# Strassen's seven products in the gate and up stages of a two-layer trunk

## The chip, the cores and the metric

The kernel runs on one core of a Trainium2 chip. A core has TensorE (PE; its weight loads, PEld, are listed apart), VectorE (DVE), ScalarE (ACT), GpSimd (POOL) and SyncE (SP, which issues most transfers here). Each engine takes its own instructions in a fixed order; semaphores hold an instruction back until its operands are there. SBUF is the working memory, PSUM the eight banks into which TensorE accumulates. The metric is the time of one execution on the device, in microseconds.

## The reference

512 tokens of 1024 features go through two layers. In each a mixer (an SSD scan in layer 0, a gated MLP over chunks of 128 tokens in layer 1) adds to the residual h, then a feed-forward stage, then a gated embedding of a second input:

```python
h = h + mix
h = h + swiglu(rmsnorm(h, norm_ffn[i]), ffn_w_gate[i], ffn_w_up[i], ffn_w_down[i])
e = rmsnorm(p[i] @ ple_w_proj[i], ple_norm[i])
gate = jax.nn.sigmoid(rmsnorm(h, ple_gate_norm[i]) @ ple_w_gate[i])
h = h + gate * e
...
def swiglu(u, w_gate, w_up, w_down):
    return (jax.nn.silu(u @ w_gate) * (u @ w_up)) @ w_down
```

All is float32. The feed-forward width is 2816, that is 22 blocks of 128 features.

## The kernel before

The residual lives feature-major in SBUF: eight tiles `H[k]` of 128 features by 512 tokens. Every large product is done as three products of a narrower float32 form: each operand is split in hi + lo, and `mm3` (lines 264 to 267) adds hi*hi, hi*lo and lo*hi in PSUM.

**Weights.** `Weights` holds all weights in the order of their use. A raw tile `wraw` (1 MB, two buffers) is loaded on SP's queue; each of its units is split by ScalarE (`whi`, line 68) and VectorE (`wlo`, line 70) into one of three hi/lo buffers, two units ahead of TensorE (`get`, with raised priority for the planner that writes out each engine's order from priorities and from the program's order). For gate and up a unit is one block: 1024 contraction rows by 128 features.

**Norm.** `Norm.block(k)` scales `H[k]` by the norm's weight, splits it into `Xh[k]`, `Xl[k]` (lines 416, 417) and adds its square to a running sum (ScalarE, then GpSimd at line 350). 1/rms of the tokens, `rs`, is multiplied into what the products give; `stat` makes it at its first use (a product with ones, a root, a reciprocal at line 283).

**Feed-forward.** `ffn` walks over the 22 blocks in parts of 8, 8 and 6, two blocks of gate and then the same two of up at a time: a round. `gemm` takes a block's 8 contraction steps, 24 matmuls of 512 columns. `on_gate` (lines 749 to 752): times rs on VectorE, silu on ScalarE, times rs on GpSimd. `on_up` (line 758): times the gate, then `split`. After each part the down product adds to h (line 606). The norm that follows takes each block of h after the last part. Between rounds, a generator (`early`) takes one step of other work: in layer 0 the norm of the embedding E and the preparation of layer 1's spatial weights, in layer 1 the second embedding.

## Time and profile before

| | |
|---|---|
| time, median of 3 runs | 1579.58 us (1577.21 to 1579.68) |
| span of the profiled execution | 1576.3 us |
| TensorE / its weight loads | 1550.5 / 1281.1 us busy |
| VectorE | 902.4 us |
| ScalarE | 644.2 us |
| GpSimd | 294.6 us |
| granted TensorE clock, mean | 0.995 of 2.4 GHz |

The span runs from the first to the last instruction of one profiled execution, for which no time beyond the span is recorded; the median of the runs lies 3.3 us above it. A busy time is the union of an engine's instructions. Matmuls overlap in the record, so the distance between two starts tells more than the duration of one.

### The profile page before, as it was taken

Reading aid. Unit: us, or ns where it says so; the run is one execution under the profiler, and the core shown is the slowest. Engines: PE = TensorE matmul, PEld = TensorE weight load, DVE = VectorE, ACT = ScalarE, POOL = GpSimd, SP = SyncE. Lnnn points to the kernel's source line nnn. Section 1 sums busy time; section 2 is a strip of 40 time slices with the busy share of each in tenths; the row PEclk is TensorE's granted clock in tenths of the full one; section 3 lists DMA queues with packets and bytes.
Section 4 is the critical chain, followed back from the end, with each engine's and each line's share of the span. In section 5 each row is a group of like instructions: output and inputs, shape, how many; then the busy total and the mean of one; then the engine's idle time right before and its main releaser. Section 6 shows DMA issues by size and latency. Waiting matters only on the chain.

```text
span 1576.3 us, 18219 instructions
## 1 busy us (share of the span) xinstructions
PE 1550.5 (98%) x7348; PEld 1281.1 (81%) x7348; DVE 902.4 (57%) x1226; ACT 644.2 (41%) x843; POOL 294.6 (19%) x226
## 2 busy tenths in 40 slices
PE   7999999999999999999999999999999999999996
PEld 5878888888878788888888888888888888888885
DVE  5679895589886433433356657535544364433445
ACT  5556663466454212222245534323343242222335
POOL 3032220123155101100124200202221001101122
PEclk9999999999999999999999999999999999999999
DMA  6463443544433323323232332332223232332231
GB/s 181 116 142 101 128 127 107 127 127 107 133 97 113 106 80 107 99 89 107 75 112 81 107 113 81 100 107 94 92 95 106 82 107 89 98 107 81 80 107 54
DMA packets 151364, 164.15 MB, mean 104 GB/s; under 512 B 5320, under 2 KB 133872, under 8 KB 151280
## 3 DMA queue, kind: packets, MB, share of 16 engines
q1 hardware_dynamic: 149648, 157.74, 33.3%
q0 software_dynamic: 1600, 5.24, 1.2%
q8 instruction: 57, 0.93, 0.2%
q14 instruction: 27, 0.22, 0.0%
q10 hardware_dynamic: 32, 0.01, 0.0%
HBM read 160.75 MB, written 2.23 MB: 103 GB/s over the span
## 4 chain that ended last, share of the span: by engine, by line
PE 88%; DVE 6%; ACT 2%; DMA 2%; SPq 1%; POOL 1%; issue 1%; ACTq 0%; DVEq 0%; POOLq 0%
PE ps L265 28%; PE ps L266 28%; PE ps L267 28%; DVE wlo L70 1%; DMA csb<-cs_dram 1%; PE ps L872 1%; PE ps L527 1%; DVE csb L576 1%; PE ps L529 1%; PE ps L260 1%; DVE acc L451 1%; PE ps L583 1%; DVE csb L511 1%; POOL sq L350 0%; DVE xsT L957 0%
## 5 line engine op out<-in xcount | busy, mean ns | idle before, releaser
L68 ACT ACTIVATE whi<-wraw 128x1024 fp32r<-128x1024 f32 (+1 forms) x270 | 279.0, 1038 | 697.6 <-PE ps L266 616.8
L265 PE MATMUL ps<-xh,whi 128*128 128x512 f32 x1120 | 441.4, 394 | 2.0 <-ACT h L400 2.0
L266 PE MATMUL ps<-xl,whi 128*128 128x512 f32 x1120 | 437.0, 390 | 2.9 <-DVE xl L398 2.0
L267 PE MATMUL ps<-xh,wlo 128*128 128x512 f32 x1120 | 436.9, 390 | 0.0
L70 DVE TENSOR_TENSOR wlo<-wraw,whi 128x1024 fp32r<-128x1024 f32 (+1 forms) x268 | 328.4, 1230 | 99.4 <-ACT whi L68 98.2
L265 PE MATMUL ps<-gh,whi 128*128 128x512 f32 x784 | 306.3, 391 | 0.0
L266 PE MATMUL ps<-gl,whi 128*128 128x512 f32 x784 | 305.0, 389 | 0.0
L267 PE MATMUL ps<-gh,wlo 128*128 128x512 f32 x784 | 304.9, 389 | 0.0
L265 PEld LDWEIGHTS ps<-xh,whi 128*128 128x128 f32 x1120 | 210.8, 188 | 48.6 <-issue 3.0
L266 PEld LDWEIGHTS ps<-xl,whi 128*128 128x128 f32 x1120 | 210.8, 188 | 47.0 <-DVE xl L398 2.5
L267 PEld LDWEIGHTS ps<-xh,wlo 128*128 128x128 f32 x1120 | 210.7, 188 | 44.5
L752 POOL TENSOR_TENSOR zs<-zs,rs 128x512 f32<-128x512 f32 x44 | 74.1, 1687 | 545.3 <-ACT zs L751 545.3
L267 PEld LDWEIGHTS ps<-gh,wlo 128*128 128x128 f32 x784 | 147.2, 188 | 30.8
L606 DVE TENSOR_TENSOR h<-h,ps 128x512 f32<-128x512 f32 x88 | 60.1, 686 | 195.7 <-PE ps L267 195.6
L265 PEld LDWEIGHTS ps<-gh,whi 128*128 128x128 f32 x784 | 147.2, 188 | 30.4 <-issue 0.3
L266 PEld LDWEIGHTS ps<-gl,whi 128*128 128x128 f32 x784 | 147.3, 188 | 30.0
L758 DVE TENSOR_TENSOR xsT<-ps,zs 128x512 f32<-128x512 f32 x44 | 30.4, 691 | 126.6 <-PE ps L267 117.8
L749 DVE TENSOR_TENSOR acc<-ps,rs 128x512 f32<-128x512 f32 x44 | 30.4, 690 | 108.2 <-PE ps L267 108.2
L350 POOL TENSOR_TENSOR sq<-sq,sq 128x512 f32<-128x512 f32 x43 | 67.7, 1574 | 128.8 <-ACT sq L347 126.8
L266 PE MATMUL ps<-wlo,gh 128*128 128x512 f32 (+1 forms) x200 | 76.3, 381 | 1.7 <-DVE wlo L70 1.7
L265 PE MATMUL ps<-whi,gh 128*128 128x512 f32 (+1 forms) x200 | 76.4, 382 | 0.0
L267 PE MATMUL ps<-whi,gl 128*128 128x512 f32 (+1 forms) x200 | 76.1, 381 | 0.0
(293 smaller groups left out, 1425.0 us busy)
## 6 DMA issues: line engine op xcount, KB each, us to landing
wraw<-in_ffn_w_gate_dram SPq DMA_DIRECT2D x22, 1024.0 KB, 5.4
wraw<-in_ffn_w_up_dram SPq DMA_DIRECT2D x22, 1024.0 KB, 5.3
wraw<-in_ssd_w_in_dram SPq DMA_DIRECT2D x16, 1024.0 KB, 5.5
wraw<-in_ffn_w_down_dram SPq DMA_DIRECT2D x16, 1024.0 KB, 5.3
wraw<-in_gmlp_w_in_dram SPq DMA_DIRECT2D x16, 1024.0 KB, 5.8
wraw<-in_ssd_w_in_dram SPq DMA_DIRECT2D x16, 512.0 KB, 4.3
csb<-cs_dram SPq DMA_DIRECT2D x32, 256.0 KB, 4.2
wraw<-in_ple_w_gate_dram SPq DMA_DIRECT2D x8, 1024.0 KB, 5.2
```

Of the source, the lines that this page charges most:

```text
L68: nc.scalar.activation(hi, src, AF.Copy)
L70: (nc.vector if n > 1 else nc.gpsimd).tensor_tensor(lo, src, f32(hi), op=ALU.subtract)
L260: nc.tensor.transpose(ps, src, ident)
L265: mm(ps, wh, xh, start=start, stop=False)
L266: mm(ps, wh, xl, start=False, stop=False)
L267: mm(ps, wl, xh, start=False, stop=stop)
L350: nc.gpsimd.tensor_tensor(sq, sq, accum, op=ALU.add)
L451: stt(a[:, d:], ps[:, : S - d], pcols[:, 0, j * 32 + b : j * 32 + b + 1], a[:, d:], op0=ALU.mult, op1=ALU.add)
L606: tt(H[m], H[m], ps, op=ALU.add)
L749: tt(a, ps, rs, op=ALU.mult)
L752: nc.gpsimd.tensor_tensor(s, s, rs, op=ALU.mult)
L758: tt(t, ps, gate[m], op=ALU.mult)
```

## The change

The gate and up products of a pair of blocks (256 features, 1024 contraction rows, 512 tokens) are taken as a 2 by 2 product of quarters in Winograd's form of Strassen's algorithm: seven products of 128 features by 512 contraction rows by 256 tokens, each of 4 steps of three matmuls of 256 columns, instead of eight. The left sides are four quarters of the raw weights (A11 to A22) and four sums S1 to S4 that GpSimd makes, one pair ahead, in tiles that before held E. The right sides are quarters of x (B11 and so on) and sums T1 to T4 that `QuarterNorm.block` makes, once a layer. The hi/lo buffers are cut in halves, one for each of the seven left sides. The results are put together from PSUM by VectorE, with one copy on ScalarE, in `after`. E is stored in DRAM and read back; its norm, the preparation of layer 1's spatial weights and layer 1's embedding move from between the rounds to behind the blocks of the last down product. In each layer's first pair, five products go side by side, three contraction steps first. The diff, cut to its core:

```diff
+PRODUCTS = (("P1", "A11", "B11"), ("P6", "S2", "T2"), ("P7", "S3", "T3"), ("P5", "S1", "T1"),
+            ("P4", "A22", "T4"), ("P2", "A12", "B21"), ("P3", "S4", "B22"))
...
+    def add_pair(self, src, col):
+        r = len(self.raws)
+        v = src.rearrange("(k p) n -> p k n", p=P)
+        self.raws.append([[(lambda t: t.rearrange("p (k n) -> p k n", n=256), v[:, :, col : col + 256])], None])
+        for _, name, _ in PRODUCTS:
+            if self.units and isinstance(self.units[-1][1], str):
+                self.at.append(self.at[-1] + 1)
+            else:
+                self.at.append(self.at[-1] // 2 * 2 + 2)
+            self.units.append((r, name))
+        self.pairs.append(r)
+    def quarters(self, r):
+        v = self.raws[r][1].rearrange("p (k t n) -> p k t n", t=2, n=256)
+        return {f"A{i + 1}{t + 1}": v[:, :, t, i * P : (i + 1) * P] for i in range(2) for t in range(2)}
+    def add_sums(self, n):
+        if n in self.sums:
+            return
+        r = self.pairs[n]
+        self._load(r)
+        a = self.quarters(r)
+        s = {}
+        for j in range(4):
+            s[f"S{j + 1}"] = self.sum_tile(4 * (n % 2) + j).rearrange("p (k n) -> p k n", n=P)
+        add = self.nc.gpsimd.tensor_tensor
+        add(s["S1"], a["A21"], a["A22"], op=ALU.add)
+        add(s["S2"], s["S1"], a["A11"], op=ALU.subtract)
+        add(s["S3"], a["A11"], a["A21"], op=ALU.subtract)
+        add(s["S4"], a["A12"], s["S2"], op=ALU.subtract)
+        self.sums[n] = s
...
+            if isinstance(view, str):
+                i = self.pairs.index(r)
+                self.add_sums(i)
+                src = (self.quarters(r) | self.sums[i])[view]
+                if self.at[n] % 2 == 0:
+                    self.half = [self.hl_pool.tile([P, 1024], F32R, tag=t, name=f"{t}{n}") for t in ("whi", "wlo")]
+                o = self.at[n] % 2 * 512
+                hi, lo = (t[:, o : o + 512].rearrange("p (k n) -> p k n", n=P) for t in self.half)
+                nc.scalar.activation(hi, src, AF.Copy)
+                nc.vector.tensor_tensor(lo, src, f32(hi), op=ALU.subtract)
+                self.tiles[n] = (hi, lo)
+                self.split += 1
+                continue
...
+        if isinstance(self.units[i][1], str):
+            r = self.units[i][0]
+            if self.units[i][1] == "A11":
+                n = self.pairs.index(r) + 1
+                if n < len(self.pairs) and self.pairs[n] == r + 1:
+                    self.add_sums(n)
+            j = i
+            while j + 1 < len(self.units) and self.at[j + 1] // 2 < self.at[i] // 2 + self.bufs:
+                j += 1
+            self._split(j)
+            self.taken += 1
+            return self.tiles.pop(i)
...
-                if i and j == 8:
-                    add_proj(1)
-                add_cols(ffn_w_gate[i], j * P, KD, 256)
-                add_cols(ffn_w_up[i], j * P, KD, 256)
+                W.add_pair(ffn_w_gate[i], j * P)
+                W.add_pair(ffn_w_up[i], j * P)
             kb = part[1] - part[0]
             for m in range(4):
+                if i and part[1] == 22 and m == 2:
+                    add_proj(1)
...
+                nc.sync.dma_start(out=e_dram[m], in_=e)
...
+                E.append(slot(f"e{m}"))
+                nc.sync.dma_start(out=E[m], in_=e_dram[m])
...
+    class QuarterNorm(Norm):
+        def __init__(self, col):
+            super().__init__(col)
+            self.extra = iter(("CT", "CT", "xdt", "xdt", "xdd", "prev", "x3", "csb", "csb", "csb", "csb", "Btok"))
+            self.right = {name: [] for _, _, name in PRODUCTS}
+            self.x = None
+        def pieces(self, k, q):
+            if q < 2:
+                return xslot(2 * k + q)
+            return [work(next(self.extra), F32R) for _ in range(2)]
+        def add(self, src, hl, names):
+            split(src, *hl)
+            for j, name in enumerate(names):
+                self.right[name].append([t[:, j * HS : (j + 1) * HS] for t in hl])
+        def block(self, k):
+            self.accum = sq_accum(H[k], self.accum, k)
+            x = work("xsT" if k % 2 else "zs")
+            act(x, H[k], AF.Identity, scale=self.col(k))
+            if k % 2 == 0:
+                self.x = x
+                return
+            xa, xb, k2 = self.x, x, k // 2
+            a1, a2, b1, b2 = xa[:, :HS], xa[:, HS:], xb[:, :HS], xb[:, HS:]
+            t23 = work("zs")
+            if k2 % 2 == 0:
+                self.t4 = work("xsT")
+            self.add(xb, self.pieces(k2, 0), ("B21", "B22"))
+            tt(t23[:, HS:], b2, a2, op=ALU.subtract)
+            tt(a2, a2, a1, op=ALU.subtract)
+            self.add(xa, self.pieces(k2, 1), ("B11", "T1"))
+            tt(t23[:, :HS], b2, a2, op=ALU.subtract)
+            self.add(t23, self.pieces(k2, 2), ("T2", "T3"))
+            nc.gpsimd.tensor_tensor(self.t4[:, k2 % 2 * HS : (k2 % 2 + 1) * HS], t23[:, :HS], b1, op=ALU.subtract)
+            if k2 % 2:
+                self.add(self.t4, self.pieces(k2, 3), ("T4", "T4"))
+    def quarter_gemm(right, copied, c2, c11, c12, first=False):
+        a, b, c = bank(), bank(), bank()
+        lo_, hi_ = slice(0, HS), slice(HS, S)
+        region = {"P1": a[:, lo_], "P6": a[:, hi_], "P7": b[:, lo_], "P5": b[:, hi_], "P4": c[:, lo_],
+                  "P2": a[:, lo_], "P3": b[:, hi_]}
+        owner = {"P1": "a", "P6": "a", "P2": "a", "P7": "b", "P5": "b", "P3": "b", "P4": "c"}
+        started = set()
+        def product(i, ws, ks):
+            n, _, name = PRODUCTS[i]
+            wh, wl = ws
+            for k in ks:
+                xh, xl = right[name][k]
+                for w, x in ((wh, xh), (wh, xl), (wl, xh)):
+                    key = owner[n]
+                    mm(region[n], w[:, k], x, start=key not in started, stop=k == 3 and w is wl, skip_group_check=True)
+                    started.add(key)
+        u, m2 = work("u"), None
+        def after(i):
+            nonlocal m2
+            n = PRODUCTS[i][0]
+            if n == "P6":
+                p1 = work("BT")[:, :HS]
+                act(p1, a[:, lo_], AF.Copy)
+                tt(u[:, lo_], a[:, hi_], p1, op=ALU.add)
+                copied()
+            elif n == "P5":
+                m2 = work("acc")
+                tt(u[:, hi_], b[:, lo_], u[:, lo_], op=ALU.add)
+                tt(m2[:, hi_], b[:, hi_], u[:, hi_], op=ALU.add)
+            elif n == "P4":
+                tt(m2[:, lo_], u[:, hi_], c[:, lo_], op=ALU.subtract)
+                c2(m2)
+            elif n == "P2":
+                c11(a[:, lo_])
+            elif n == "P3":
+                c12(b[:, hi_], u[:, lo_])
+        if first:
+            ws = [W.get() for _ in range(5)]
+            for ks in (range(3), range(3, 4)):
+                for i in range(5):
+                    product(i, ws[i], ks)
+            for i in (1, 3, 4):
+                after(i)
+        for i in range(5 if first else 0, 7):
+            product(i, W.get(), range(4))
+            after(i)
...
-    nf = Norm(lambda k: pcol(16 + k))
+    nf = QuarterNorm(lambda k: pcol(16 + k))
...
-    def ffn(norm, after, early):
+    def ffn(norm, after, late):
+        lo_, hi_ = slice(0, HS), slice(HS, S)
         for pi, (b0, b1) in enumerate(FFN_PARTS):
             for j in range(b0, b1, 2):
-                if norm.rs is not None:
-                    next(early, None)
-                gate = [None, None]
-                def on_gate(m, ps):
+                gate = [work("zs"), work("zs")]
+                def gate2(t):
                     rs = norm.rstd()
-                    a = work("acc")
-                    tt(a, ps, rs, op=ALU.mult)
-                    s = work("zs")
-                    act(s, a, AF.Silu)
-                    nc.gpsimd.tensor_tensor(s, s, rs, op=ALU.mult)
-                    gate[m] = s
-                def on_up(m, ps):
+                    tt(t, t, rs, op=ALU.mult)
+                    act(gate[1], t, AF.Silu)
+                    nc.gpsimd.tensor_tensor(gate[1], gate[1], rs, op=ALU.mult)
+                m1 = work("acc")
+                def gate11(ps):
+                    tt(m1[:, lo_], ps, norm.rstd()[:, lo_], op=ALU.mult)
+                def gate12(ps, u):
+                    rs = norm.rstd()
+                    tt(m1[:, hi_], ps, u, op=ALU.add)
+                    tt(m1[:, hi_], m1[:, hi_], rs[:, hi_], op=ALU.mult)
+                    act(gate[0], m1, AF.Silu)
+                    nc.gpsimd.tensor_tensor(gate[0], gate[0], rs, op=ALU.mult)
+                up = []
+                def put(m):
                     k = j - b0 + m
-                    t = work("xsT")
-                    tt(t, ps, gate[m], op=ALU.mult)
                     GH[k], GL[k] = gslot(k)
-                    split(t, GH[k], GL[k])
-                gemm(2, KD, Xh, Xl, on_gate, outer=2 if j == 0 else 0)
-                gemm(2, KD, Xh, Xl, on_up)
+                    split(up[m], GH[k], GL[k])
+                def up2(t):
+                    up.extend((work("xsT"), work("xsT")))
+                    tt(up[1], t, gate[1], op=ALU.mult)
+                    put(1)
+                def up11(ps):
+                    tt(up[0][:, lo_], ps, gate[0][:, lo_], op=ALU.mult)
+                def up12(ps, u):
+                    t = work("acc")
+                    tt(t[:, hi_], ps, u, op=ALU.add)
+                    tt(up[0][:, hi_], t[:, hi_], gate[0][:, hi_], op=ALU.mult)
+                    put(0)
+                quarter_gemm(norm.right, (lambda: norm.rstd()), gate2, gate11, gate12, first=j == 0)
+                quarter_gemm(norm.right, (lambda: None), up2, up11, up12)
             def on_down(m, ps, last=pi == 2):
                 add_h(m, ps)
                 if last:
                     after(m)
+                    next(late, None)
...
-        next(finish_e)
+        finish_e()
+        for j in range(4):
+            ws_raw.append(work(("xdt", "xdt", "xdd", "x3")[j]))
+            bsb.append(work(("prev", "CT", "csb", "csb")[j]))
+            nc.gpsimd.dma_start(out=ws_raw[j].rearrange("t (g s) -> t g s", s=P), in_=gmlp_w_s[0, 4 * j : 4 * j + 4].rearrange("g t s -> t g s"))
+            nc.gpsimd.dma_start(out=bsb[j].rearrange("q (g t) -> q g t", t=P),
+                                in_=gmlp_b_s[0, 4 * j : 4 * j + 4].partition_broadcast(P))
+        wsT.extend(work(t) for t in ("csb", "csb", "cbm", "Btok"))
```

## Rows read from the trace of the kernel before

**Rows 1.** The page, busy us (share of the span) and instructions of each engine:

```profile
PE 1550.5 (98%) x7348; PEld 1281.1 (81%) x7348; DVE 902.4 (57%) x1226; ACT 644.2 (41%) x843; POOL 294.6 (19%) x226
```

**Rows 2.** Timeline of TensorE, 1554 to 1566: start, duration, engine, line, instruction:

```profile
1554.71 0.39 PE L266 MATMUL ps<-wlo,gh 128*128 128x512 f32 x1
...
1561.06 0.39 PE L267 MATMUL ps<-whi,gl 128*128 128x512 f32 x1
1561.28 0.28 PE L265 MATMUL ps<-whi,gh 128*128 128x256 f32 x1
...
1565.48 0.28 PE L267 MATMUL ps<-whi,gl 128*128 128x256 f32 x1
```

**Rows 3.** Timeline of the weight loads in the same stretch:

```profile
1561.40 0.19 PEld L267 LDWEIGHTS ps<-whi,gl 128*128 128x128 f32 x1
1561.52 0.19 PEld L265 LDWEIGHTS ps<-whi,gh 128*128 128x128 f32 x1
```

**Rows 4.** Windows: four rounds of layer 0, and around its last down product:

```profile
core 0: us, PE busy (x) PEld busy (x) DVE busy (x) ACT busy (x) POOL busy (x), PEclk, DMA share, GB/s
600.50:687.50 87.00, 87.00 (x386) 72.06 (x385) 34.08 (x39) 24.02 (x30) 14.32 (x8) 1.00 0.31 97
780.00:835.00 55.00, 55.00 (x244) 45.54 (x243) 27.66 (x34) 23.21 (x32) 12.24 (x8) 1.00 0.27 86
```

**Rows 5.** Groups by shape, VectorE: count | busy us, mean ns | idle before:

```profile
L271 DVE TENSOR_TENSOR gl<-xsT,gh 128x512 fp32r<-128x512 f32 x22 | 15.0, 682 | 0.7 <-ACT gh L270 0.7
L606 DVE TENSOR_TENSOR h<-h,ps 128x512 f32<-128x512 f32 x88 | 60.1, 686 | 195.7 <-PE ps L267 195.6
L587 DVE TENSOR_TENSOR x<-x,ps 128x256 f32<-128x256 f32 x8 | 3.4, 420 | 1.8 <-POOL x L586 1.5
```

**Rows 6.** Timeline of VectorE and GpSimd at three places:

```profile
455.63 1.87 DVE L606 TENSOR_TENSOR h<-h,ps 128x512 f32<-128x512 f32 x3
455.90 1.30 POOL L350 TENSOR_TENSOR sq<-sq,sq 128x512 f32<-128x512 f32 x1 [0.74 <-ACT sq L347]
...
847.04 0.74 DVE L417 SCALAR_TENSOR_TENSOR gl<-h,pcols,gh 128x512 fp32r<-128x512 f32 x1
847.71 1.21 DVE L70 TENSOR_TENSOR wlo<-wraw,whi 128x1024 fp32r<-128x1024 f32 x1
848.27 1.80 POOL L350 TENSOR_TENSOR sq<-sq,sq 128x512 f32<-128x512 f32 x1 [2.30 <-ACT sq L347]
848.84 1.78 DVE L417 SCALAR_TENSOR_TENSOR gl<-h,pcols,gh 128x512 fp32r<-128x512 f32 x1
...
1062.67 1.29 POOL L876 TENSOR_TENSOR CT<-CT,u 128x512 f32<-128x512 f32 x1 [53.68 <-DVE CT L874]
```

**Rows 7.** Timeline of VectorE in a down product:

```profile
809.81 0.69 DVE L606 TENSOR_TENSOR h<-h,ps 128x512 f32<-128x512 f32 x1 [1.80 <-PE ps L267]
810.47 0.96 DVE L70 TENSOR_TENSOR wlo<-wraw,whi 128x768 fp32r<-128x768 f32 x1
811.34 0.74 DVE L417 SCALAR_TENSOR_TENSOR xl<-h,pcols,xh 128x512 fp32r<-128x512 f32 x1
813.89 0.69 DVE L606 TENSOR_TENSOR h<-h,ps 128x512 f32<-128x512 f32 x1 [1.80 <-PE ps L267]
```

**Rows 8.** Groups by shape over the whole span:

```profile
L283 DVE RECIPROCAL rs<-rs 128x512 f32<-128x512 f32 x13 | 43.5, 3347 | 3.8 <-ACT rs L282 3.8
L270 ACT ACTIVATE gh<-xsT 128x512 fp32r<-128x512 f32 x22 | 13.9, 630 | 5.7 <-DVE xsT L758 5.4
```

**Rows 9.** Timeline of VectorE and TensorE where layer 0's feed-forward begins:

```profile
447.68 1.27 DVE L606 TENSOR_TENSOR h<-h,ps 128x512 f32<-128x512 f32 x2
...
454.73 0.39 PE L265 MATMUL ps<-xh,whi 128*128 128x512 f32 x1
...
464.19 0.50 PE L266 MATMUL ps<-xl,whi 128*128 128x512 f32 x1 [0.91 <-DVE xl L417]
```

**Rows 10.** The chain that ended last, the same place: start, us, what:

```profile
460.07 1.31 POOL sq L350
462.11 1.48 POOL sq L350
464.32 1.64 POOL sq L350
```

**Rows 11.** The page, transfers issued: count, KB each, us to landing:

```profile
wraw<-in_ffn_w_gate_dram SPq DMA_DIRECT2D x22, 1024.0 KB, 5.4
```

**Rows 12.** Timeline of SP's queue in a round:

```profile
622.95 0.37 SPq L52 DMA_DIRECT2D wraw<-in_ffn_w_up_dram  x1
633.83 0.37 SPq L52 DMA_DIRECT2D wraw<-in_ffn_w_gate_dram  x1
```

More of the change, by code (lines that the diff above doesn't have):

```diff
@@ L15 @@
 S = 512
+HS = 256
 DM = 1024
@@ L339, in finish @@
             for m in range(8):
+                E.append(slot(f"e{m}"))
+                nc.sync.dma_start(out=E[m], in_=e_dram[m])
+            for m in range(8):
                 nc.gpsimd.tensor_tensor(E[m], E[m], rs, op=ALU.mult)
-            yield
-        return E, finish()
+        return E, finish
     def sq_accum(src, accum, k, scale=1.0 / 32):
@@ L816, in spatial @@
         yield
-    ffn(nf, npg.block, early=spatial())
+    ffn(nf, npg.block, spatial())
     xh, xl = Xh, Xl
@@ L888, in trunk @@
         gemm(8, 8, GH, GL, on_out, outer=2)
[L891 to L896 removed]
+    we, wf, E, spare = [], [], [], []
     sums = cp.tile([P, 2, NCH, 3], F32, name="sums")
```

41 lines of the change are left out of this document (20 added, 21 removed).

## The prediction

> **What bounds the kernel now.** Read the busy times first: TensorE is busy in 98% of the span, VectorE in 57%, ScalarE in 41%, GpSimd in 19% [rows 1]. A busy TensorE need not be at its peak, so the next view is its order of instructions. In the stream of 512-column products one starts every (1561.06 - 1554.71) / 28 = 0.2268 us with nothing between, and at the very end, where one block is cut in two, 36 products of 256 columns start every (1565.48 - 1561.28) / 35 = 0.120 us, each with a weight load of its own in the same rhythm [rows 2, 3]. The granted clock stays at the upper level (2.4 GHz, 1.00 in the rows) through the feed-forward stages, where TensorE fills the whole stretch and VectorE 34 of 87 us [rows 4]. So TensorE's columns set the time there, and taking an eighth of them away is worth something exactly as long as no other engine becomes the bound.
>
> One round of `ffn` (a gate pair and an up pair of blocks) takes 96 x 0.2268 = 21.77 us; there are 11 rounds a layer, 22 in all, in parts of 4, 4 and 3 rounds with a down product after each.
>
> **The change part by part.** *TensorE.* A round becomes 2 x 7 products x 12 matmuls = 168 of 256 columns: 168 x 0.120 = 20.16 us. Gain 1.61 x 22 = 35.3 us. It is less than an eighth because the 256-column product carries the same fixed part: (0.120 x 2 - 0.2268) = 13 ns. For weight loads of 128x128 the record shows 188 ns, more than 120, but they start every 0.12 us [rows 3], so they overlap and cost nothing further.
> By the Trainium skill ("TensorE: Matmul & The Clock Gate", What overlaps and what doesn't) a weight load runs beside a matmul only where the row groups differ, which these don't; by its figure of 107 ns a load, an estimate, a round would be longer by 168 x 0.107 = 18 us. The trace disagrees: 0.120 us holds load and product. It is a rival below.
>
> *VectorE.* Instructions of 512 elements take 0.685 us, from SBUF or from PSUM, and of 256 elements 0.42 [rows 5]; back to back one of 512 starts every (1.87 - 0.68) / 2 = 0.60 us [rows 6], and one of 256, with the same 0.08 of overlap, every 0.34. A gate pair now has 7 `wlo` (4.2 us), seven 256-wide additions and multiplications in `after`, `gate11`, `gate12` (2.38) and one 512-wide in `gate2` (0.60): 7.18. An up pair has the same 4.2 and 2.38, `up2` (0.60) and two `lo` halves of `split` (1.2): 8.38. A round: 15.56 us of 20.16, where the rows of before show 34.08 us in four rounds, 8.5 each [rows 4].
>
> *GpSimd.* `add_sums` adds four 128x512 additions to a pair; with the two multiplications by rs a round has 10, where it had 2. One alone takes 1.29 us [rows 6].
>
> *What the two cost each other* decides the case. A GpSimd addition and a VectorE instruction with two SBUF inputs do not run together. At 848.27 a GpSimd addition starts while a `wlo` runs: it takes 1.80 us, the `wlo` its normal 1.21; the next VectorE instruction, normally 0.74, takes 1.78 [rows 6]. So VectorE lost 1.04 us to it. Instructions that read PSUM don't: the three at 455.63 run in 1.87 us straight through a GpSimd addition [rows 6].
> The Trainium skill ("SBUF — State Buffer", SBUF: two separate sides) calls this an exclusive lock on the pair's shared port, held for a whole instruction; by that, with 1.29 us a time, VectorE would lose a quarter more than by the row. The row decides.
>
> Of a round's 32 VectorE instructions 20 have two SBUF inputs (14 `wlo`, `gate2`, `up2`, two `lo`, two of 256) and 12 read PSUM. Where a PSUM one stands next in the queue it runs while GpSimd holds the port, and hides its 0.34. Following the order of the calls, with one `wlo` between products, that is so behind 5 of 9 instructions in a gate pair and 5 of 11 in an up pair, once with two in a row: (4 x 0.34 + 0.68) / 9 = 0.23 and / 11 = 0.19, on average 0.21. So the loss w is 1.04 - 0.21 = 0.83 us a GpSimd instruction. Its bounds: 1.04 (nothing hidden) and 0.40 (all 12 PSUM instructions of a round always hide: 12 x 0.34 / 10 = 0.41 less, and waits in which VectorE would have stood idle anyway).
>
> Can VectorE keep up? In a part of 4 rounds it must finish the `wlo` of the 56th product before TensorE comes to it, after 55 x 1.44 = 79.2 us. Its work up to there: 4 x 15.56 = 62.2, less 3.8 that follows that `wlo` and runs under the down product, less 1.8 for three `wlo` made during the last down block (those phases leave VectorE free: [rows 7] show waits of 1.80 us in every block): 56.6. GpSimd has 7 x 4 sums (the first pair's are made earlier) and 8 multiplications, 36: w may be 22.6 / 36 = 0.63. In a part of 3 rounds: 46.7 - 5.6 = 41.1 of 41 x 1.44 = 59.0 us, 26 instructions, 0.69. At w = 0.83 the parts are late by 56.6 + 29.9 - 79.2 = 7.3 and 41.1 + 21.6 - 59.0 = 3.7 us: 4 x 7.3 + 2 x 3.7 = 36.6 us. That eats the 35.3: +1.3.
> Each layer's first part also has the reciprocal of rs, 3.35 us on VectorE [rows 8], so far under its idle time: +6.6.
>
> *Start of the first feed-forward stage.* `QuarterNorm.block` replaces, for two blocks, two 0.66 instructions (the L417 form) by three 256-wide and 3.5 splits: 1.02 + 2.1 = 3.1 us of VectorE, and 3.5 more activations. Before, TensorE goes on without a gap at 454.73 and waits 0.91 once, at 464.19, for VectorE [rows 9]; the chain that ended last runs there over GpSimd's squares [rows 10]. The eight blocks come in 2 x 24 x 0.2268 = 11 us. From the first addition to h at 447.68 [rows 9] VectorE has, up to the six blocks that the first product needs: 6 x 0.60 + 3 x 3.1 + 1.2 + five `wlo` 3.0 = 17 us, and 6 squares and 4 sums on GpSimd at up to 1.04 = up to 10. So it is ready at 465 to 475, and TensorE waits 10 to 20 us, less what is done in a better order. I take +12 (6 to 20).
> *Start of the second.* The blocks come one per 5.44 us, so only the last one's chain counts: add, scale, split, difference, split, difference, split, T4's, some 9 us at 0.6 to 0.7 each, of which three quarters of the first five products (5.4 us) cover all but 3 (1 to 6).
>
> *What is moved behind the last down product:* E's norm (8 GpSimd multiplications), w_s's transposes and products, in layer 1 p's embedding. TensorE has the same work. VectorE had 27.7 of 55 us there [rows 4]; it gets one reciprocal, 4 masks and 16 short ones, some 10 us, and up to 8 x 1.04 of waits, against 32.6 us of down product. +4 for both layers (0 to 10). E's way through DRAM is 16 transfers of 256 KB; issuing takes 0.37 us on SP's queue, where weight loads queue behind them; those land in 5.4 us and are issued every 10.9 [rows 11, 12], so this cover is 5 us a time, and I cost it at nothing. ScalarE, at 0.63 us a 512-wide instruction (0.55 back to back) [rows 8], gets 7 x 0.55 + 0.4 + 1.1 = 5.4 us a pair of 10: nothing.
>
> Sum: 1.3 + 6.6 + 12 + 3 + 4 = +27 us. The profiled span is 1576.3, the median of the runs 1579.58, 3.3 more, which I leave as it is: 1579.6 + 27 = 1606.
>
> **The rivals.** *TensorE stays the bound* (the other side): the waits on the port fall under PSUM instructions or idle time, w below 0.63. For it: 12 PSUM instructions a round, and that GpSimd has only 10 x 1.64 = 16.4 us of work in 20.16, so it needn't press always. Against: sums come in bursts of four. Then -35.3 + 12 + 3 + 4 = -16: 1563; with the low ends (7) 1551. Chance 0.25.
> *No cover:* w = 1.04. Parts are late by 56.6 + 37.4 - 79.2 = 14.8 and 41.1 + 27.0 - 59.0 = 9.1: 77.4 - 35.3 + 6.6 + 19 = +68, with the high ends (36) +85: 1647 to 1665. For it: the order of the queues is fixed and doesn't know of the port. Chance 0.12.
> *Weight loads don't overlap:* a 256-column product takes 0.188, the recorded load. 168 x 0.188 = 31.6 a round, +9.8 x 22 = +216: 1795. Against it stands [rows 3]. Chance 0.02.
> *Gain and losses cancel* to within 0.2% (3.2 us, about what a measurement of this kernel can tell from no change): w near 0.70. Chance 0.05.
>
> **How the numbers follow.** The forecast, VectorE held up by the port sets the pace of the rounds, has 0.56, with 1585 to 1640 of its own. Slower: 0.56 + 0.12 + 0.02 = 0.70; same 0.05; faster 0.25. The range must reach into the faster rival: 1560 leaves out somewhat less than half of it (0.11), 1648 most of the worse ones (0.09).
>
> **What would show it.** Right: in the rounds 256-column products every 0.120 us with gaps that end with `wlo` on VectorE; VectorE above 85% busy, `wlo` of 128x512 at a mean near 1.0 us and not 0.69; a round of 22 to 23.5 us late in a part, shorter at its beginning; a gap of about 12 us near 455. Wrong: `wlo` near 0.7 and TensorE without gaps (the first rival), or gaps that end with GpSimd's sums or products spaced wider than 0.120, which this sum doesn't contain.

## The result, and the profile after

The changed kernel took 1662.45 us (median of 4 runs, 1661.13 to 1663.53) against 1578.39 for the kernel before: a ratio of 1.0534, 95% interval 1.0519 to 1.0549. The forecast was 1606 in 1560 to 1648: the direction was right, the size three times too small (+84 us for +27).

The busy times, as in [rows 1], now read:

```profile
PE 1549.7 (93%) x8932; PEld 1346.9 (81%) x8932; DVE 1262.4 (76%) x1746; ACT 749.1 (45%) x1131; POOL 562.3 (34%) x410
```

TensorE is no longer full, and VectorE, at 76% over the whole span, looks far from full too. The window of one steady part, the second part of layer 0, says otherwise; the second line is the beginning of layer 0's first part. Columns as in [rows 4].

```profile
621.20:716.30 95.10, 84.50 (x674) 82.64 (x673) 91.09 (x122) 41.99 (x77) 51.10 (x32) 0.98 0.28 89
460.00:480.00 20.00, 7.42 (x22) 5.36 (x23) 18.89 (x24) 15.18 (x27) 12.66 (x10) 0.50 0.00 0
```

Those four rounds took 87.0 us before and were to take 80.6; they take 95.1, with VectorE busy 91.1 of it where it was 34 in [rows 4]. In the beginning TensorE runs 22 matmuls in 20 us, at its lower clock (0.50).

VectorE's groups by shape (count | busy us, mean ns | idle before), beside [rows 5]:

```profile
L121 DVE TENSOR_TENSOR wlo<-e,whi 128x512 fp32r<-128x512 f32 x176 | 195.8, 1116 | 12.3 <-ACT whi L120 12.3
L121 DVE TENSOR_TENSOR wlo<-wraw,whi 128x512 fp32r<-128x512 f32 x132 | 134.0, 1020 | 5.0 <-ACT whi L120 4.8
...
L937 DVE TENSOR_TENSOR acc<-acc,rs 128x256 f32<-128x256 f32 x22 | 23.3, 1060 | 0.0
...
L577 DVE TENSOR_TENSOR u<-ps,BT 128x256 f32<-128x256 f32 x44 | 18.2, 413 | 0.0
```

The same 256 elements cost 1.06 us where both inputs lie in SBUF (L937) and 0.41 where one lies in PSUM (L577). The timeline of VectorE, GpSimd and TensorE in a round shows how (a choice of its lines), beside [rows 6]:

```profile
658.05 1.74 POOL L94 TENSOR_TENSOR e<-wraw 128x512 f32<-128x512 f32 x1
658.57 1.51 DVE L937 TENSOR_TENSOR acc<-acc,rs 128x256 f32<-128x256 f32 x1
659.75 1.48 POOL L93 TENSOR_TENSOR e<-e,wraw 128x512 f32<-128x512 f32 x1
660.00 1.78 DVE L121 TENSOR_TENSOR wlo<-wraw,whi 128x512 fp32r<-128x512 f32 x1
661.71 1.78 DVE L121 TENSOR_TENSOR wlo<-e,whi 128x512 fp32r<-128x512 f32 x1
663.41 0.41 DVE L577 TENSOR_TENSOR u<-ps,BT 128x256 f32<-128x256 f32 x1
663.88 0.39 PE L566 MATMUL ps<-xh,whi 128*128 128x256 f32 x1 [1.00 <-DVE u L577]
665.10 1.76 DVE L121 TENSOR_TENSOR wlo<-e,whi 128x512 fp32r<-128x512 f32 x1
666.78 0.41 DVE L581 TENSOR_TENSOR u<-ps,u 128x256 f32<-128x256 f32 x1
667.23 0.42 DVE L582 TENSOR_TENSOR acc<-ps,u 128x256 f32<-128x256 f32 x1
667.71 0.38 PE L566 MATMUL ps<-xh,whi 128*128 128x256 f32 x1 [2.14 <-DVE acc L582]
```

While GpSimd adds without a pause, the two engines alternate: a `wlo` takes 1.4 to 1.78 instead of 0.69. The evictions L577 to L582 are short, but stand in the queue behind the `wlo`, and TensorE waits for them to give a bank back. So over the whole span TensorE's waits (us, times, longest) are led by evictions, not by `wlo`:

```profile
PE ps L566 <- DVE u L577: 27.7, 23, 2.0
PE ps L566 <- DVE acc L582: 22.8, 17, 2.1
PE ps L566 <- ACT xh L348: 12.1, 3, 6.0
PE ps L566 <- DVE wlo L121: 6.5, 7, 2.3
```

The third is the start of layer 0, beside [rows 9]. The timeline there:

```profile
454.12 1.29 POOL L92 TENSOR_TENSOR e<-wraw 128x512 f32<-128x512 f32 x1
...
458.13 1.44 POOL L430 TENSOR_TENSOR sq<-sq,sq 128x512 f32<-128x512 f32 x1
459.60 0.63 ACT L427 ACTIVATE sq<-h 128x512 f32<-128x512 f32 x1 [3.52 <-POOL sq L430]
461.93 0.58 PE L566 MATMUL ps<-xh,whi 128*128 128x256 f32 x1 [6.03 <-ACT xh L348]
469.67 0.58 PE L566 MATMUL ps<-xh,whi 128*128 128x256 f32 x1 [5.32 <-ACT xh L348]
```

The second pair's sums (from L92) stand on GpSimd's queue ahead of a block's square (L430), for which ScalarE waits 3.52 us with the splits `xh` behind it.

Where the time went, by stage: us from the first product of a stage to the first of the next, worked out from the timelines of TensorE. "Start 0" is w_out's last 48 products with layer 0's first part. Before, it held 5.2 us of work that the change moves behind the last down product (E's 1/rms 0.5, transposes 1.7, products with ones 3.0), and layer 1's first part held 0.8 (transposes).

| kernel | start 0 | 2nd part | 3rd | layer 1: first | 2nd | 3rd |
|---|---|---|---|---|---|---|
| before | 106.0 (100.8 + 5.2) | 87.0 | 65.3 | 88.4 (87.6 + 0.8) | 87.0 | 65.3 |
| after | 132.8 | 95.1 | 70.9 | 106.7 | 95.8 | 69.8 |
| TensorE's pace | 91.5 | 80.6 | 60.5 | 80.6 | 80.6 | 60.5 |

Nearly everything lies in these six parts; the rest is +6.4 us around the two last down products beyond the moved work; what is left elsewhere is within 1 us.

### The profile page after: what moved, and what is told of

Read it like the earlier page. It is cut to its first block, busy times and chain, and to the rows that moved or that the text cites. A ratio compares the mean times of both kernels' runs of the same rounds, so it can differ in the third digit from the quotient of the medians.

```text
span 1660.9 us, 22623 instructions
## 1 busy us (share of the span) xinstructions
PE 1549.7 (93%) x8932; PEld 1346.9 (81%) x8932; DVE 1262.4 (76%) x1746; ACT 749.1 (45%) x1131; POOL 562.3 (34%) x410
## 4 chain that ended last, share of the span: by engine, by line
PE 67%; DVE 21%; issue 5%; ACT 3%; DMA 3%; POOL 2%; SPq 0%; POOLq 0%; DVEq 0%; ACTq 0%
PE ps L343 17%; PE ps L344 17%; PE ps L345 17%; PE ps L566 12%; DVE wlo L121 8%; DVE acc L937 1%; PE ps L704 1%; DVE wlo L133 1%; PE ps L1075 1%; DVE xl L349 1%; DVE rs L361 1%; DVE acc L582 1%; DVE u L577 1%; PE ps L706 1%; DVE xsT L959 1%
## 5 line engine op out<-in xcount | busy, mean ns | idle before, releaser
L343 PE MATMUL ps<-xh,whi 128*128 128x512 f32 x768 | 304.3, 397 | 1.9 <-ACT h L480 1.9
L344 PE MATMUL ps<-xl,whi 128*128 128x512 f32 x768 | 300.2, 391 | 2.0 <-DVE xl L478 2.0
L345 PE MATMUL ps<-xh,wlo 128*128 128x512 f32 x768 | 300.2, 391 | 0.0
L133 DVE TENSOR_TENSOR wlo<-wraw,whi 128x1024 fp32r<-128x1024 f32 (+1 forms) x180 | 222.0, 1239 | 74.1 <-ACT whi L131 72.3
L121 DVE TENSOR_TENSOR wlo<-e,whi 128x512 fp32r<-128x512 f32 x176 | 195.8, 1116 | 12.3 <-ACT whi L120 12.3
L343 PE MATMUL ps<-gh,whi 128*128 128x512 f32 x432 | 169.9, 395 | 0.0
L344 PE MATMUL ps<-gl,whi 128*128 128x512 f32 x432 | 168.2, 390 | 0.0
L345 PE MATMUL ps<-gh,wlo 128*128 128x512 f32 x432 | 168.2, 390 | 0.0
L92 POOL TENSOR_TENSOR e<-wraw 128x512 f32<-128x512 f32 x44 | 64.1, 1457 | 285.7 <-DMA wraw<-in_ffn_w_gate_dram 142.2
L566 PE MATMUL ps<-xh,whi 128*128 128x256 f32 x352 | 105.0, 298 | 38.0 <-DVE u L577 13.2
L121 DVE TENSOR_TENSOR wlo<-wraw,whi 128x512 fp32r<-128x512 f32 x132 | 134.0, 1020 | 5.0 <-ACT whi L120 4.8
L566 PE MATMUL ps<-gh,whi 128*128 128x256 f32 x352 | 104.2, 297 | 29.6 <-DVE u L577 14.5
L430 POOL TENSOR_TENSOR sq<-sq,sq 128x512 f32<-128x512 f32 x43 | 62.9, 1462 | 118.2 <-ACT sq L427 118.2
```

What stands on the lines that cost most here:

```text
L92: add(s["S1"], a["A21"], a["A22"], op=ALU.add)
L121: nc.vector.tensor_tensor(lo, src, f32(hi), op=ALU.subtract)
L133: (nc.vector if n > 1 else nc.gpsimd).tensor_tensor(lo, src, f32(hi), op=ALU.subtract)
L343: mm(ps, wh, xh, start=start, stop=False)
L344: mm(ps, wh, xl, start=False, stop=False)
L345: mm(ps, wl, xh, start=False, stop=stop)
```

## The experiments

My theory after the result: GpSimd's sums, through the port, make VectorE the engine that sets the pace; the rest is a slow start of each layer. Rivals: VectorE's own added work without the port; the burst in which the sums come; too few PSUM banks; too short a lead of the split weights. The edits are cut to the lines that matter. e1, e4, e6 and e9 leave sums out and so give other values: they show what the sums cost, and are no kernels to use.

**The sums left out, done by VectorE, or replaced by a write.**

```
-        add(s["S1"], a["A21"], a["A22"], op=ALU.add)      # and S2, S3, S4
+        s = {"S1": a["A21"], "S2": a["A22"], "S3": a["A11"], "S4": a["A12"]}   # e1
-        add = self.nc.gpsimd.tensor_tensor
+        add = self.nc.vector.tensor_tensor                                     # e2, e3
-                nc.gpsimd.tensor_tensor(gate[1], gate[1], rs, op=ALU.mult)     # and gate[0]
+                nc.vector.tensor_tensor(gate[1], gate[1], rs, op=ALU.mult)     # e3
+            self.nc.gpsimd.memset(s[f"S{j + 1}"], 0.25)                        # e4, for the sums
```

> The four sums of a pair are left out: S1 to S4 stand for the quarters A21, A22, A11, A12 themselves; GpSimd has 2 additions a round instead of 10, and VectorE, ScalarE and TensorE have exactly what they had in the changed kernel. Port theory (VectorE's two-input instructions wait for GpSimd's, some 29 us in a part of four rounds): the 128x512 wlo falls from a mean near 1.07 us to below 0.75 in the rounds, VectorE's work in a part of four rounds from 91 to about 70 us, the part becomes TensorE's: 80.6 to 83 us instead of 95, three rounds 60.5 to 62 instead of 70; the starts of both stages lose their share of sums too, the whole 1570 to 1600 us. Rival, VectorE is overloaded by its own 32 instructions a round and the additions are only beside it: parts stay at 93 to 95 us, the whole above 1640. Second rival, the two starts cost most of the loss: the parts gain as the port theory says, but the first parts stay 20 and 18 us above before, so the whole is not below 1600.

> The four sums of a pair are made by VectorE instead of GpSimd, the same values. VectorE gets 8 more instructions of 0.60 us in a round, 4.8 us. Port theory: each addition on GpSimd costs VectorE 0.8 to 1.04 us, so 0.60 on VectorE itself is cheaper: a part of four rounds takes 62.2 + 28 x 0.60 + 8 x 0.9 = 86 to 89 us instead of 95, the whole 1615 to 1640. Rival, VectorE's own count is the trouble: a part gets 17 us longer, 110 us, the whole above 1710.

> As the run before, and the two multiplications by rs of a round on VectorE too: GpSimd does nothing in the rounds, VectorE 42 instructions where it had 32. Port theory: no waits are left, a part of four rounds is 62.2 + 28 x 0.60 + 8 x 0.60 = 84 us of VectorE, 83 to 86 us long; wlo at 0.68; the whole 1605 to 1630, faster than the run before by 5 to 15 us. Rival, VectorE's count: slower than the run before, 115 us a part.

> GpSimd writes a constant into the four tiles of the sums instead of adding: as many GpSimd instructions, the same waits of other engines for them, but nothing read. The sums are left out. If what holds VectorE up is that GpSimd reads SBUF through the shared port: wlo near 0.70 us, parts of 81 to 83 us, as without the sums. If any GpSimd instruction in the way does it (the writes, or the order of the semaphores): wlo stays above 0.85 and the parts above 88.

Measured: e1 1567.51 us, ratio 0.9918 (0.9886 to 0.9950); e2 1621.54, 1.0260 (1.0224 to 1.0295); e3 1620.50, 1.0253 (1.0219 to 1.0288); e4 1568.77, 0.9926 (0.9897 to 0.9955). The window of the second part, in e1, e2, e3 and e4:

```profile
596.60:677.10 80.50, 80.50 (x673) 80.50 (x672) 69.51 (x123) 42.92 (x77) 10.34 (x8) 1.00 0.34 105
```

```profile
614.46:701.31 86.85, 82.61 (x674) 81.16 (x672) 83.33 (x146) 43.12 (x77) 11.85 (x8) 1.00 0.31 97
```

```profile
612.53:697.31 84.78, 81.84 (x674) 80.92 (x672) 80.75 (x154) 42.21 (x76) 0.00 (x0) 1.00 0.33 100
```

```profile
598.72:679.35 80.63, 80.63 (x674) 80.63 (x672) 69.78 (x123) 42.97 (x77) 25.41 (x37) 1.00 0.34 105
```

Without the sums TensorE has no gap. With the sums on VectorE the part takes 86.85, 8 us less than with GpSimd's help: an addition costs VectorE 0.60 us of its own time, (83.33 - 69.51) over 23 more instructions than in e1, and 0.90 when GpSimd makes it, (91.09 - 69.51) over the 24 sums that lie in the changed kernel's window. In e3 GpSimd is idle, VectorE has 80.75 us of undisturbed work, and the part still takes 4.0 more than that; the whole, expected 5 to 15 us under e2, comes out only 1.0 under. e4 puts a GpSimd instruction where each sum was, one that writes as much and reads nothing; VectorE's busy time is that of e1. Its groups by shape:

```profile
L92 POOL MEMSET e<- 128x512 f32 x176 | 92.1, 527 | 391.7 <-DVE wlo L118 368.4 <-ACT whi L117 16.0 <-PE ps L1072 5.0
...
L118 DVE TENSOR_TENSOR wlo<-e,whi 128x512 fp32r<-128x512 f32 x176 | 136.5, 779 | 20.9 <-ACT whi L117 19.5
```

The mean `wlo` is 0.78 us, as in e1 (0.777; in e3, with GpSimd idle in the rounds, 0.68 to 0.69). So it is not that GpSimd works, but that it reads SBUF. By the Trainium skill ("SBUF — State Buffer", SBUF: two separate sides) a VectorE instruction with two SBUF inputs is locked out only by a GpSimd one that reads SBUF; e4 agrees, with 0.779 us.

**Spreading the sums; a fourth bank; a longer lead.**

```
-    def add_sums(self, n):
+    def add_sums(self, n, upto=4):            # e5: one sum is queued per product
-        "P6": a[:, hi_]
+        "P6": d[:, lo_]                       # e7: P6 gets a bank of its own
-                i = self.pairs.index(r)       # e14: line 113 no longer overwrites
+                p = self.pairs.index(r)       #      the bound of _split's loop
```

> The same four sums on GpSimd, but queued one by one over the products of the pair before instead of all four at its first product, so that they no longer come in one run with the two multiplications by rs. Burst theory (VectorE's lag in a burst of six outruns the two to three products that a PSUM bank can wait, and that makes TensorE and then VectorE idle): the loss of VectorE in a part stays near 29 us, but TensorE's waits for the additions that read PSUM shrink; a part of four rounds 88 to 92 us instead of 95, the whole 1625 to 1650. Rival, the sum of VectorE's work alone decides (91 us busy of 95): parts stay at 93 to 96, the whole within 8 us of 1662. Second rival, spread additions find VectorE's PSUM instructions beside them and hide: loss below 20 us, parts below 86.

> P6 gets a PSUM bank of its own, so that P2, which adds into P1's bank, no longer waits for VectorE's reading of P6. Bank theory (TensorE's waits are 5.7 us for that addition and 4.6 for the ones before P3 in a part of four rounds): the first kind goes, a part takes 89 to 92 us, which is VectorE's own 91 busy us; the whole 1635 to 1650. Rival, the waits only stand where TensorE happens to meet VectorE's lag: they move to P3 and to wlo, parts stay at 94 to 96, the whole within 8 us of 1662.

> All the work is kept; the halves of the weights may be split up to six products ahead of TensorE, as the three buffers of whi and wlo allow. In the kernel as changed a loop bound in _split (line 112 writes its result over i) lets only one product's halves be split at each call, so the lead that a part starts with is never built up. If VectorE's total decides (my reading so far), only the halves made during the down product before a part can help: three or four more of them, 0.7 us each on a free VectorE and about 1 us each inside a part, so each of six parts is shorter by 3 to 4 us and the time by 15 to 25 us: 1638 to 1648. If the lead was the cause of the lateness altogether, parts of four rounds fall to the 80.6 us of TensorE's pace: below 1590. If evictions alone make TensorE wait and the lead doesn't matter: 1660 to 1664. The start of a layer may get worse, as VectorE has more to do before the first product.

Measured: e5 1663.97 us, 1.0530 (1.0483 to 1.0577); e7 1666.67, 1.0547 (1.0516 to 1.0579); e14 1667.42, 1.0562 (1.0548 to 1.0577). The second part takes 95.3, 95.2 and 96.3. e5 decides little: the sums wait for their tile's transfer and came in runs all the same, so the burst stays untested as a cause of its own. In e7 the wait for L577 is gone from the list of waits and another has taken its place:

```profile
PE ps L566 <- DVE acc L582: 45.3, 19, 3.5
```

In the changed kernel the two were 27.7 + 22.8. In e14 I expected 15 to 25 us less and got 5 more. Its window:

```profile
621.62:717.94 96.32, 84.92 (x673) 82.69 (x672) 92.01 (x122) 41.95 (x77) 50.38 (x32) 0.98 0.28 88
```

VectorE is as full as before, and TensorE waits for the evictions (L577 42.4 us, `wlo` 2.1). But the edit didn't give the lead that it was to test. Counted in the two timelines, four halves are split when the first product of a layer's second part starts, with the edit and without; over the part, 2.1 halves not yet used up are ready on average when a product starts, in both. So the loop's bound is not what limits the lead, and what a longer lead would be worth is not shown.

**The T sums left out, alone and with the S sums.**

```
-            tt(t23[:, HS:], b2, a2, op=ALU.subtract)      # and the rest of T1 to T4 with their splits
+            for name, of in (("T2", "B11"), ("T3", "T1"), ("T4", "B21")):
+                self.right[name].append(self.right[of][-1])
```

> The right sides' sums T1 to T4 are left out: the quarters of x stand for them, so that the norm of two blocks makes two splits instead of three and a half, no difference and no GpSimd addition; the rounds have the same instructions. If the sums T cost the start: layer 0's first part with the wait before it (6.2 + 115.7 us) falls by 8 to 14 us, layer 1's (106.7) by 2 to 5; the whole 1645 to 1652. Rival, the start is slow because the next pair's sums hold GpSimd and with it the squares, ScalarE and VectorE: less than 4 us in both, the whole above 1656.

> Neither the sums of the weights nor those of x are made (quarters stand for both): seven products at no price but their own splits and the putting together. Rounds: 80.6 and 60.5 us a part. First parts: 98.6 us without the weights' sums alone; if the sums of x are what is left, layer 0's falls to 86 to 91 and layer 1's from 84.3 to 81 to 83, the whole 1550 to 1558. Rival, it is the reciprocal and the wait for rs: within 3 us of 98.6, the whole 1562 to 1568.

Measured: e6 1648.99 us, 1.0435 (1.0400 to 1.0471): 7.3 us less in layer 0's start, 6.5 in layer 1's, the parts behind them unchanged. e9: 1559.32, 0.9868 (0.9839 to 0.9897). e6 keeps to the range of the whole, with less than expected in layer 0 and more in layer 1; e9 ends 1.3 us above its range. So the two sets of sums together cost 103 us, and the S sums are 90 of them, once the T sums are gone.

**All the work kept, but one input of `wlo` moved out of SBUF.** This tests the port itself: GpSimd keeps every sum, and ScalarE, which has time, copies hi into PSUM, from where VectorE subtracts it.

```
-                nc.vector.tensor_tensor(lo, src, f32(hi), op=ALU.subtract)
+                hp = self.bank().rearrange("p (k n) -> p k n", n=P)      # e10: 1 bank, e11: 2
+                nc.scalar.activation(hp, f32(hi), AF.Copy)
+                nc.vector.tensor_tensor(lo, src, hp, op=ALU.subtract)
```

> All of the changed kernel's work stays, GpSimd's sums too; ScalarE copies each quarter's hi half into one PSUM bank kept for it, and VectorE takes the wlo from SBUF and PSUM, so that it has one SBUF input and no longer waits for GpSimd. One bank fewer for everything else, 56 more ScalarE copies of 0.55 us in a part (43 to some 74 of 95 us). Port theory: wlo near 0.69 us; VectorE's work in a part of four rounds from 91 to near 70 us; the part 80.6 to 87 (the one bank makes each wlo wait for the copy before it), three rounds 60.5 to 66, the whole 1585 to 1625. Rival, VectorE's own count or GpSimd's lateness with the sums: parts stay at 93 or more, the whole above 1650.

> The same with two banks for the hi copies and six for the rest. Port theory: copies run ahead of wlo, a part is TensorE's: 80.6 to 82 us, three rounds 60.5 to 62; stages that want eight banks (the start, layer 1's first products) lose up to 10 us in all; the whole 1580 to 1605, and the first parts keep 15 and 4 us of their start. Rival as in the run before: parts of 93 or more. Second rival: with ScalarE near full the whi copies come late and TensorE waits for them: parts of 84 to 90 with ScalarE above 85% busy.

Measured: e10 1657.43 us, 1.0493 (1.0478 to 1.0509); e11 1586.12, 1.0046 (1.0029 to 1.0062). e10 misses its range, 1585 to 1625: with one bank the copy and the subtraction take turns, and TensorE waits 41.1 us for `wlo`. With two, the groups by shape of e11:

```profile
L122 ACT ACTIVATE hp<-whi 128x512 f32<-128x512 f32 x308 | 176.7, 588 | 12.7 <-DVE wlo L123 10.8
L123 DVE TENSOR_TENSOR wlo<-e,hp 128x512 fp32r<-128x512 f32 x176 | 119.1, 680 | 19.6 <-ACT hp L122 19.0
L123 DVE TENSOR_TENSOR wlo<-wraw,hp 128x512 fp32r<-128x512 f32 x132 | 88.4, 681 | 36.9 <-ACT hp L122 36.6
```

The timeline of e11 where GpSimd adds without a pause:

```profile
639.63 0.69 DVE L123 TENSOR_TENSOR wlo<-wraw,hp 128x512 fp32r<-128x512 f32 x1 [0.59 <-ACT hp L122]
639.68 1.30 POOL L95 TENSOR_TENSOR e<-wraw,e 128x512 f32<-128x512 f32 x1
640.94 1.31 POOL L930 TENSOR_TENSOR zs<-zs,rs 128x512 f32<-128x512 f32 x1
641.16 0.69 DVE L123 TENSOR_TENSOR wlo<-e,hp 128x512 fp32r<-128x512 f32 x1 [0.51 <-ACT hp L122]
```

And its window of the second part:

```profile
606.18:686.81 80.63, 80.63 (x673) 80.63 (x672) 67.96 (x123) 69.59 (x129) 44.79 (x32) 1.00 0.34 105
```

`wlo` is back at 0.68, GpSimd's addition takes 1.30, and TensorE has no gap, with all the sums made. That settles the steady parts. What is left of e11's loss lies in the two first parts (117.0 and 93.3) and in the output stage, 2.2 us longer with six banks.

**The starts, on top of e11.** e12: the first pair of a layer makes no copies in PSUM. e13: and the second pair's sums are queued later. e17: e12 with e14's lead. e18: e11 with the additions of E's squares on VectorE. e19: both e12 and e18. e20: e18, and the output stage takes the copies' two banks. e21: e20 with the squares of `QuarterNorm.block` on VectorE.

```
+                if i % 22:                                                   # e12: around the copy
-            if self.units[i][1] == "A11":
+            if self.units[i][1] == ("A12" if first else "A11"):              # e13
-                    nc.gpsimd.tensor_tensor(accum, accum, sq, op=ALU.add)
+                    tt(accum, accum, sq, op=ALU.add)                         # e18
-        pss = [bank() for _ in parts]
+        pss = [(bank if nt or i > 1 else W.bank)() for i in range(len(parts))]   # e20
-            self.accum = sq_accum(H[k], self.accum, k)
+            self.accum = sq_accum(H[k], self.accum, k, add=tt)               # e21
```

> e11 (copies of hi in PSUM, all the work kept), but the first gate pair of each layer takes its wlo from SBUF as before, without ScalarE's seven copies of 0.59 us, since ScalarE's chain of splits is what TensorE waited for there (9.2 of 18.5 us in e11). If ScalarE's total sets the start, each layer's first part is shorter by 2 to 4 us: 1579 to 1582, the same as the kernel before. If GpSimd's squares set it, no change: 1586.

> As e12_start, and the second pair's four sums of each layer are queued on GpSimd after the first five products' weights and not ahead of them, so that the squares of the last blocks don't stand behind them. In the changed kernel ScalarE waited 3.5 us there for a square that stood behind these sums. If that wait was on the path, 2 to 4 us less than e12_start in the first layer: 1576 to 1580. If not, equal to e12_start within 1 us.

> As e12_start, with the longer lead of e14_lead. Without the port's wait VectorE has 5 us to spare in a part, so the lead should matter little inside the parts, which are at TensorE's pace already (80.63 and 60.47): equal to e12_start within 2 us, or some us slower if the halves split early hold up the start of a layer.

> As e11 (copies of hi in PSUM, all the work kept), and the seven additions of E's squares (line 416 of e11) move from GpSimd to VectorE. In e11 GpSimd is busy 19.84 of the 20 us from 440 to 460, at 1.29 us for each of these, with the first two pairs' sums between them, and ScalarE's splits stand behind the squares; VectorE is busy only 11.42 there. If GpSimd's queue is what delays the first part, about 6 to 9 us come off: 1577 to 1580, the same as the kernel before or faster. If not, 1586.

> As e18_esq_vec with e12_start's edit (no PSUM copies for the first pair of a layer). If the two delays add up, another 1 to 2 us less than e18: 1576 to 1579. If GpSimd's sums then take the port from these wlo, equal to e18 or 1 us more.

> As e18 (all the work kept), and the output stage's first four products use the two PSUM banks that the copies of hi no longer need by then. In e11 and e18 the stage took 52.18 us with six banks, 50.0 with eight. If the banks are what it waits for, 2 us less than e18: 1578 to 1579, equal to the kernel before or just faster. If not, 1580.6.

> As e20, and the additions of the squares in QuarterNorm.block (eight a layer, 1.3 to 1.7 us each on GpSimd) are made by VectorE (0.6 each), so that ScalarE's squares and the splits behind them do not wait for GpSimd's queue: in e11 ScalarE waited 4.3 us for one of them in layer 1, behind sums that waited for their weights' DMA. If that queue still delays the first parts, 3 to 6 us less than e20: 1573 to 1576. If VectorE's own work there (18 to 19 of 20 us busy from 460 to 500) decides, 1 to 4 us more than e20.

| kernel | us | ratio (95%) | start 0 | layer 1: first |
|---|---|---|---|---|
| e11 | 1586.12 | 1.0046 (1.0029 to 1.0062) | 117.0 | 93.3 |
| e12 | 1584.74 | 1.0042 (1.0030 to 1.0055) | 118.8 | 92.7 |
| e13 | 1587.74 | 1.0055 (1.0041 to 1.0068) | 120.3 | 92.6 |
| e17 | 1604.10 | 1.0158 (1.0144 to 1.0172) | 120.4 | 95.4 |
| e18 | 1580.63 | 1.0006 (0.9998 to 1.0015) | 113.3 | 92.4 |
| e19 | 1583.54 | 1.0028 (1.0018 to 1.0037) | 116.1 | 92.8 |
| e20 | 1577.62 | 0.9986 (0.9977 to 0.9995) | 113.0 | 92.4 |
| e21 | 1577.15 | 0.9983 (0.9974 to 0.9992) | 114.3 | 90.2 |

e12, e13 and e19 miss: their edits leave the start as it was or lengthen it. So neither ScalarE's copies nor the second pair's sums, behind which ScalarE waited 3.52 us above, set it by themselves. e17 misses by far: its second parts take 83.5 and 84.1 where e12's take 80.6. Its lead is no longer than e12's (2.4 and 2.3 halves ready on average in the two second parts, for 2.8), so it is again no test of a longer one; why the parts are slower was not settled. e18 hits the place. The windows from 440 to 460, of e11 and then of e18:

```profile
440.00:460.00 20.00, 16.63 (x74) 13.45 (x72) 11.42 (x15) 10.30 (x19) 19.84 (x16) 0.99 0.40 132
```

```profile
440.00:460.00 20.00, 15.72 (x66) 12.36 (x65) 19.93 (x26) 12.19 (x23) 15.54 (x11) 0.93 0.30 107
```

GpSimd, full in e11, has room, and start 0 falls by 3.7 us, where I expected 6 to 9: VectorE is now full in its place. e20's two banks give the output stage its 50.0 back. e21 shortens layer 1's first part by 2.2 us and lengthens layer 0's by 1.3, where VectorE is short; in all no difference from e20 that the runs can tell. e20 and e21 keep all the work and end just below the kernel before, by an amount that lies within the 0.2% taken as no change.

## Why the prediction was wrong in size

*TensorE* was right: 256-column products start every 0.120 us with a weight load each, and wherever VectorE keeps up a part of four rounds takes 80.63 us (4 x 20.16).

*The port* was right as a mechanism and in its total. In the steady part of the window above, VectorE's 122 instructions at what the same forms take of its time in e3, where GpSimd is idle (0.60 us for 512 elements, 0.34 to 0.35 for 256), make 61.4 us; it was busy 91.1. The rest is 29.7, and the forecast had 29.9. But the forecast had it as 36 GpSimd instructions of 0.83 us, and the window holds 32 (the second pair's sums, too, are made before the part begins), which makes 0.93 us each. The price was too low and the count too high, and that the two cancel is luck. e1, e4 and e11 show from three sides that the port is the cause. The PSUM evictions do pass beside GpSimd (0.41 to 0.42), as assumed.

*The step that failed* is the one headed "Can VectorE keep up?": the balance "62.2, less 3.8 that follows that `wlo` and runs under the down product, less 1.8 for three `wlo` made during the last down block: 56.6". It makes a part late only by what VectorE's work up to the last `wlo` exceeds TensorE's 79.2 us, as if VectorE never stood idle before that `wlo` and nothing but that `wlo` held TensorE up. The work came out right: in the second part of layer 0 VectorE is busy 87.2 us from the part's first matmul to the end of the last `wlo`, for 56.6 + 29.9 = 86.5. But 3.9 us of idle time bring that end to 91.1, and the part ends 4.0 us after it, where the balance has one product left, 1.44. The three longest idle stretches:

```profile
624.85 0.69 DVE L121 TENSOR_TENSOR wlo<-e,whi 128x512 fp32r<-128x512 f32 x1 [1.58 <-ACT whi L120]
627.13 0.42 DVE L581 TENSOR_TENSOR u<-ps,u 128x256 f32<-128x256 f32 x1 [0.66 <-PE ps L566]
...
710.89 1.38 DVE L121 TENSOR_TENSOR wlo<-e,whi 128x512 fp32r<-128x512 f32 x1 [0.61 <-ACT whi L120]
```

The first two come before VectorE is late at all: six halves, as many as the three hi/lo buffers hold, are split by then, and ScalarE's next `whi` starts at 624.18, when TensorE is through the first two products. In e3, without any port, the same two take 1.52 and 0.71. So VectorE can't run ahead of TensorE as far as the balance has it; whether a fourth buffer would help was not tried. The 4.0 at the end I put down to the evictions: of TensorE's waits in this part 10.3 us end with them and 0.3 with a `wlo`, the last one nine products before the end, and TensorE is then more than one product behind when the last `wlo` is done. So what follows a `wlo` in VectorE's queue counts as well. That it is not the bank that P6 shares is shown by e7, where it has its own and the part is as long. In the four steady parts the last `wlo` is done 3.1 to 5.2 us later than the balance has it, and the end follows 2.6 to 3.7 us later than one product. In place of 7.3 and 3.7 late against TensorE's pace, the parts are late by 14.5 and 15.1 (four rounds) and 10.4 and 9.3 (three): 49.3 for 22.0, +27. For the first parts I take the same error once each, +7 and +7; this is not taken apart, but VectorE is as full there, 97% and 96% (layer 0, then layer 1):

```profile
461.93:577.63 115.70, 91.77 (x674) 86.29 (x675) 112.07 (x153) 58.85 (x104) 64.23 (x42) 0.91 0.24 74
1194.11:1300.78 106.67, 89.86 (x676) 86.73 (x674) 102.33 (x134) 51.04 (x89) 59.49 (x39) 0.94 0.25 80
```

*The starts* were mis-sized too. Start 0 is 41.3 us above TensorE's pace, 2.9 of which it had before, for a forecast of 12 + 3.35 + 7.3 = 22.7; without the 7 just counted that leaves +8.5. Layer 1's first part is 26.0 above, 0.6 of it before, for 13.7: +4.5. The forecast priced VectorE's chain, counted six squares and four sums as a loss of VectorE's, and left out that E's squares, the first two pairs' sums and the blocks' squares share GpSimd's queue, with ScalarE's splits behind the squares: in e18 seven of these additions off that queue take 3.7 us off. What the T sums add is 7 us a layer (e6). Of the rest of start 0 (21.5 us above the pace in e20, 2.9 in the kernel before) I have not shown the cause part by part.

*What is moved behind the last down product* costs 6.4 us for +4, within the 0 to 10 given.

Together: +27 forecast, +27 steady, +14 in the first parts' rounds, +13 for the starts, +2 for what is moved make +83; measured 84.1 in the medians.

*The rivals.* "TensorE stays the bound" gave 1563 and is what e9 (1559) and e1 (1568) look like, with the sums left out; with all the work, TensorE sets the pace of the steady parts as soon as the port is not in the way (e11). "No cover", 1647 to 1665, contains the measured time, but not for its reason: w was 0.93 over 32 instructions, not 1.04 over 36. "Weight loads don't overlap" is ruled out by 80.63 us a part. Of the signs named, `wlo` near 1.0 and VectorE above 85% came true. The sign "gaps that end with `wlo`" did not: they end with evictions, a dependence that the balance had left out.

## What to carry to other kernels

An engine that stands between two others sets the pace well before its busy share reaches 100%: count all of its work in the stage, evictions too, and allow some 5% on top (4.0 of 84.8 us in e3, 4.0 of 95.1 in the changed kernel) before you trust that it keeps up. When help from GpSimd slows VectorE by more than the work it takes over (0.90 us a piece for 0.60), look whether one of VectorE's two inputs can come from PSUM; here ScalarE had the 0.59 us a tile to put it there, and that took 76 us off. A change that takes columns from TensorE for sums elsewhere pays only as far as those engines have room at the stage's worst place, its start included: even repaired, seven products for eight came out even.

## What the runs showed of the hardware

A GpSimd instruction that only writes (0.527 us for 128x512) leaves `wlo` at 0.779 (0.777 in e1, where those instructions are gone); one that reads SBUF makes it 1.02 to 1.12 on average and up to 1.78. With one input in PSUM VectorE (0.68) and GpSimd (1.30) run together undisturbed.

Behind a gap TensorE also lost clock. The windows around the 2.14 us gap that ends at 667.71 in the changed kernel:

```profile
666.00:668.00 2.00, 0.29 (x2) 0.30 (x3) 1.94 (x4) 0.00 (x0) 0.97 (x2) 0.99 0.20 64
668.00:670.00 2.00, 2.00 (x11) 2.00 (x11) 1.92 (x2) 0.63 (x1) 2.00 (x2) 0.50 0.00 0
670.00:672.00 2.00, 2.00 (x14) 2.00 (x13) 2.00 (x3) 1.15 (x2) 2.00 (x2) 0.66 0.00 0
```

The granted clock falls to its lower level (0.50, 1.2 GHz) behind the gap: 17 matmuls take 3.59 us from 667.71 to 671.30 instead of 2.04, so TensorE lost 3.7 us to a wait of 2.1. Where VectorE sets the pace, the kernel need not lose it: e7's second part has a mean clock of 0.93 and is as long (95.19) as that of the changed kernel with 0.98 (95.10):

```profile
622.09:717.28 95.19, 87.16 (x674) 86.36 (x673) 90.94 (x122) 42.74 (x77) 50.55 (x32) 0.93 0.29 89
```
